# A transformer trunk on one core: context's w2 sums kept in PSUM, the mixing norm of token group 1 taken step by step, raw weights in nineteen tiles

## The chip, the core and the metric

The kernel runs on one core of a Trainium2 chip. The metric is the device time of one execution in microseconds (us), lower is better. The core has TensorE (PE, matrix products; its weight loads are listed as PEld), VectorE (DVE), ScalarE (ACT), GpSimd (POOL), and SyncE (SP), whose queue issues nearly all DMAs. Matrix products add up in PSUM: eight banks of 128 partitions x 512 floats, in two rings of four tiles, psa and psb.

## The reference

One layer of a diffusion backbone on 1024 latent tokens and 256 context tokens, model width 1024, hidden width 2816. Cut to what matters:

```python
x   = x   + 0.5 * m_l[2] * swiglu(modulate(rms_norm(x,   norm1_w), m_l[0], m_l[1]), w1, w3, w2)
ctx = ctx + 0.5 * m_c[2] * swiglu(modulate(rms_norm(ctx, norm1_w), m_c[0], m_c[1]), w1, w3, w2)
y_l, _ = token_mixing(modulate(rms_norm(x, norm2_w), m_l[3], m_l[4]),
                      modulate(rms_norm(ctx, norm2_w), m_c[3], m_c[4]), ...)
x = x + m_l[5] * y_l
x = x + 0.5 * m_l[8] * swiglu(modulate(rms_norm(x, norm3_w), m_l[6], m_l[7]), v1, v3, v2)
return rms_norm(x, final_norm_w)

def swiglu(h, w1, w3, w2):
    return (silu(h @ w1) * (h @ w3)) @ w2
```

Token mixing has retention heads and gated linear attention heads. The retention decay uses `log_sigmoid` of eight numbers per layer.

## The kernel before, in words

Activations lie transposed: x[tg][k] is 128 features x the tokens of group tg. Groups 0 and 1 are 512 latent tokens each, group 2 is the 256 context tokens. Every product is made of three matmuls in a reduced float format: each operand is split into a high part (hi, made by ACT, line 60) and a low part (lo, the rest, by DVE or POOL, line 61), and `mm3` (lines 63 to 67) adds hi x hi, hi x lo and lo x hi.

The first FFN of the latent tokens uses a seven-product scheme: products of hidden blocks are stored to memory (gd), and `back6` and `prod` (lines 466, 493) make the w2 products from them. The last of these, prod(4), is left for later.

Between back6 and prod(4) lies the **context's hidden stage**, the loop at line 1575: eleven passes, each on a pair of hidden blocks f and f + 1, through `classic` (line 621). For each block it loads w1 and w3 in halves of 128 x 512 (`load_halves`, `load_half`, `raw_half`), splits them, makes `H` (line 616: 24 matmuls of 256 columns into one psa bank), then silu (`s1`, ACT), the product (`s3`, DVE), and its split into g. Two pairs of hi and lo tiles of a half are taken from the slots h00 to h07 (`halves_slots`, line 274), in turn. In the middle of each pass `mid2` makes the w2 sums of the pass before: `Y` (line 591) takes four half-weights of w2, split by DVE, and for each of the eight feature blocks six matmuls into a psb bank, after which DVE multiplies by the gate and adds to x[2] (line 600). The w1 and w3 halves' low parts are made by POOL here (CENG). The last sums, Y(20), are put into prod(4) by a plan of steps (`plan`, lines 1505 to 1548), and the context's second norm after them.

All raw weight halves land in a ring of NR = 6 tiles ("raw", line 258). The pool of f1 has another ring, "s", of 19 tiles of the same size (`stile`, line 575), which holds silu's results and the kept products.

In the same passes the norm of token group 1 for the mixing stage is made: `norm2(1, i)` (lines 1516 to 1535). Step 0 sums squares, step 1 sums over features with small matmuls (line 187) and takes the power on POOL, step 2 spreads the result over the partitions with small matmuls (line 203) and copies it, and the steps 3 to 10 write h[1][k]: DVE at line 217, ACT at 218, DVE at 223. One step is handed over after each pass (`pend`), but h[1] is allocated whole ahead of them (line 1572), and its small sums use psb (psN).

After prod(4) come the norm of group 0, the context's keys and values (`ctx_k`, `ctx_v`), and `mix_setup` (line 873), which calls `lg_setup` (line 840): it loads the eight decays, makes log_sigmoid with a power on POOL and a series of some 25 tiny DVE instructions, and from it the tables kd and cdec (ACT). Then the mixing stage, the output projection and the second FFN.

Within each engine the order of the instructions is made by a scheduler that goes by priorities in program order (`high_priority`, `low`) and by its own estimate of when things are ready; at some places an order is fixed by hand. It also assigns the tiles of a ring and adds the waits. Each engine runs its queue in order.

Of the kernel before, what the change touches and what calls it, by code (L numbers as in the profile page):

```python
# [11 lines left out]
F32 = mybir.dt.float32  # L12
F32R = mybir.dt.float32r
AF = mybir.ActivationFunctionType
ALU = mybir.AluOpType
PSUM = bass.MemoryType.PSUM

P = 128
D = 1024
KD = D // P  # L20
DFF = 2816
NF = DFF // P
NP = NF // 2
LAT = 1024
CTX = 256
# [6 lines left out]
class Trunk:  # L32
# [222 lines left out]
                          for k in range(KD)]  # L255

    def raw_half(self, src=None):
        t = self.tile(self.wp, [P, 512], F32, "raw", NR)
        if src is not None:
            t = t[:, :src.shape[1]]  # L260
            self.nc.sync.dma_start(t, src)
        return t
# [11 lines left out]
    def halves_slots(self, i):  # L274
        if i < 2:
            return None, None
        return tuple(self.hslot(f"0{2 * (i % 4) + j}") for j in range(2))

    def load_halves(self, src, dst=(None, None), eng=None):
        return [self.load_half(src[:, 512 * i:512 * i + 512], dst[i], eng) for i in range(2)]  # L280
# [212 lines left out]
    def back6(self, keep=True):  # L493
        A = self.bank4(self.psA)
        self.prod(1, A, True)
        c1 = self.keep4(A)
        B = self.bank4(self.psB)
        self.prod(2, B, True)
        self.add4(0, 0, self.plus4(c1, B))
        self.prod(6, A, False)  # L500
        u2 = self.keep4(A)
        B = self.bank4(self.psB)
        self.prod(5, B, True)
        c5 = self.keep4(B)
        self.prod(7, A, False)
        if keep:
            u3 = self.keep4(A)
            self.add4(1, 1, self.plus4(c5, u3))
        else:
            self.add4(1, 1, self.plus4(c5, A))  # L510
            self.add4(0, 1, A)
        self.prod(3, B, False)
        self.add4(1, 0, self.plus4(u2, B))
        return A
# [54 lines left out]
    def ffn_open(self, i, gates, pool):  # L569
        self.w1, self.w3, self.w2 = (self.I[f"w{i}{j}"] for j in (1, 3, 2))  # L570
        self.gates_m, self.fp, self.s, self.g = gates, pool, {}, {}
        self.gd, self.sd = self.gds[i - 1], self.sds[i - 1]
        self.nraw, self.nslot, self.feed, self.steps, self.held = -1, 0, iter(()), None, None

    def stile(self):
        return self.tile(self.fp, [P, 512], F32, "s", self.ns)
# [14 lines left out]
    def Y(self, f, order, after=None, qs=(0, 1)):  # L591
        nc, g = self.nc, self.g

        def unit(w, tg, o, n, m):
            ps = self.psB()
            for i in range(2):
                self.mm3(ps[:, :n], [t[:, m % 4 * P:(m % 4 + 1) * P] for t in w[i]], [t[:, o:o + n] for t in g[f + i, tg]],
                         i == 0, i == 1)
            x = self.x[tg][m][:, o:o + n]
            nc.vector.scalar_tensor_tensor(out=x, in0=ps[:, :n], scalar=self.gates_m[int(tg == 2)][:, m:m + 1], in1=x,  # L600
                                           op0=ALU.mult, op1=ALU.add)

        ws = {}
        for q in qs:
            ws[q] = [self.load_half(self.w2[f + i][:, 512 * q:512 * q + 512]) for i in range(2)]
            if not after:
                for tg, o, n in order:
                    for m in range(4):
                        unit(ws[q], tg, o, n, 4 * q + m)
        if after:  # L610
            for tg, o, n in order:
                for m in range(KD):
                    unit(ws[m // 4], tg, o, n, m)
                after(tg, o, n)

    def H(self, w, tg):
        ps = self.psA()
        self.proj(w, tg, ps)
        return ps
# [217 lines left out]
            act(a, a, AF.Exp, scale=-1.0)  # L837
            act(a, a, AF.Ln, bias=1.0)

    def lg_setup(self):  # L840
        nc, I, cp = self.nc, self.I, self.cp2
        x = self.tile(cp, [P, 8], F32, "lgx")
        nc.sync.dma_start(x, I["decay"].broadcast_to([P, 8]))
        e = self.tile(cp, [P, 8], F32, "lge")
        nc.vector.memset(e, float(np.e))
        u = self.tile(cp, [P, 8], F32, "lgu")
        nc.vector.tensor_scalar(out=u, in0=x, scalar1=-1.0, scalar2=None, op0=ALU.mult)
        nc.vector.tensor_tensor(out=u, in0=u, in1=x, op=ALU.min)
        nc.gpsimd.tensor_tensor(out=u, in0=e, in1=u, op=ALU.pow)
        t = self.tile(cp, [P, 8], F32, "lgt")  # L850
        nc.vector.tensor_scalar(out=t, in0=u, scalar1=2.0, scalar2=None, op0=ALU.add)
        nc.vector.reciprocal(t, t)
        nc.vector.tensor_tensor(out=u, in0=u, in1=t, op=ALU.mult)
        nc.vector.tensor_tensor(out=t, in0=u, in1=u, op=ALU.mult)
        nc.vector.tensor_scalar(out=e, in0=t, scalar1=1.0 / 19, scalar2=1.0 / 17, op0=ALU.mult, op1=ALU.add)
        for m in (15, 13, 11, 9, 7, 5, 3, 1):
            nc.vector.tensor_tensor(out=e, in0=e, in1=t, op=ALU.mult)
            nc.vector.tensor_scalar(out=e, in0=e, scalar1=1.0 / m, scalar2=None, op0=ALU.add)
        nc.vector.tensor_tensor(out=e, in0=e, in1=u, op=ALU.mult)
        nc.vector.tensor_scalar(out=x, in0=x, scalar1=0.0, scalar2=None, op0=ALU.min)  # L860
        nc.vector.scalar_tensor_tensor(out=x, in0=e, scalar=-2.0, in1=x, op0=ALU.mult, op1=ALU.add)
        self.lg = x
        self.kd = {}
        for i, (nm, s, pos) in enumerate((("f", 0, 2), ("f0", 0, 3), ("b", 4, 0), ("b1", 4, 1))):
            t = self.tile(cp, [P, 4], F32, "kd" + nm)
            nc.vector.tensor_scalar(out=t, in0=x[:, s:s + 4], scalar1=self.tab[:, POSC + pos:POSC + pos + 1],
                                    scalar2=None, op0=ALU.mult)
            nc.scalar.activation(t, t, AF.Exp)
            self.kd[nm] = t
        self.cdec = self.tile(cp, [P, 8], F32, "cdec")  # L870
        nc.scalar.activation(self.cdec, x, AF.Exp, scale=float(P))
# [572 lines left out]
    def run(self):  # L1444
        nc, tc, I = self.nc, self.tc, self.I
        S = {}

        def opn(name, side="left"):
            S[name] = tc.tile_pool(name=name, bufs=1, reuse_waits="tile", side=side)
            return S[name].__enter__()  # L1450
# [9 lines left out]
        xp = opn("xp", "right")  # L1460
        self.x, self.h, self.tr = {}, {}, None
        self.consts()
        warm = self.tile(self.dp, [P, 8], F32, "warm")
        nc.scalar.activation(warm, self.mhalf, AF.Silu)
        self.load_x((xp, xp, None), (0,))
        nc.scalar.activation(self.ccol, self.ccol, AF.Silu)
# [6 lines left out]
        with tc.manual_schedule(engines={mybir.EngineType.PE, mybir.EngineType.DVE, mybir.EngineType.Activation}):  # L1473
            ws = self.first1((xp, xp, None), n1)
# [24 lines left out]
        hc = opn("hc", "right")  # L1499
        self.gp = hc  # L1500
        n2 = opn("n2", "right")
# [3 lines left out]
        plan = defaultdict(list)  # L1505
# [10 lines left out]
        def norm_step(tg, i, a, b):  # L1516
            with self.low(NLOW if tg == 1 and i in (1, 2) else None):
                norm_part(tg, i, a, b)
# [16 lines left out]
        norm2 = lambda tg, i: norm_step(tg, i, self.mcol(4, int(tg == 2)), self.mcol(3, int(tg == 2)))  # L1535
        for i, at in enumerate((24, 27, 30, *range(33, 33 + KD))):
            plan[at].append(lambda i=i: ctx1(i))

        CT = [(2, 0, 256)]
        p4 = 6 * NP  # L1540
        plan[p4 + 1] += [lambda: self.Y(NF - 2, CT), lambda: self.alloc_h((2,), hc), lambda: norm2(2, 0)]
        plan[p4 + 4].append(lambda: norm2(2, 1))
        plan[p4 + 6].append(lambda: norm2(2, 2))
        for k in range(KD):
# [22 lines left out]
        def spill(tg):  # L1567
            o = TGS[tg][0]
            for k in range(KD):
                nc.sync.dma_start(self.xd[k * P:(k + 1) * P, o:o + 512], self.x[tg][k])  # L1570

        self.alloc_h((1,), self.hp)
        norm2(1, 0)
        pend = [lambda i=i: norm2(1, i) for i in range(1, 3 + KD)] + [lambda: spill(1)]
        for f in range(0, NF, 2):
            self.classic(f, (2,), mid2=(lambda: self.Y(f - 2, CT)) if f else None, eng=[nc.gpsimd if e else None for e in CENG])
            pend.pop(0)()
        A = self.bank4(self.psA)
        self.prod(4, A, True)
        self.add4(0, 1, A)  # L1580
# [48 lines left out]
        raw = [self.t34_raw(k) for k in range(4)]  # L1629
# [18 lines left out]
NR = 6  # L1648
# [17 lines left out]
CENG = (1, 1, 1, 1)  # L1666
# [98 lines left out]
```

## Time and profile before

| | us |
|---|---|
| median of 3 runs | 2178.55 |
| lowest and highest run | 2176.82, 2179.85 |
| profiled execution | 2180.54 |
| its span in the profile | 2178.8 |
| PE busy | 2121.3 (97% of the span) |
| DVE busy | 1525.0 (70%) |
| ACT busy | 980.7 (45%) |
| POOL busy | 280.4 (13%) |

The profile is of one execution. A row of a timeline has the start, the length, the engine and line, the operation, the tile written and the tiles read, and in brackets the idle time of the engine ahead of it and what ended that. A row of waits has who waited, for whom, the sum, the count and the longest. A group has its count, the busy time, the mean length of one in ns, and the idle time ahead of it. A table of stages has the busy time of each engine in a stretch, and PEclk, the clock that was granted to TensorE as a share of full speed. Lengths of matmuls are modelled; the pace of PE is read from the distance of their starts.

### The profile page before, as it was taken

Reading aid. Unit: us, or ns where it says so; the run is one execution under the profiler, and the core shown is the slowest. Engines: PE = TensorE matmul, PEld = TensorE weight load, DVE = VectorE, ACT = ScalarE, POOL = GpSimd, SP = SyncE. Lnnn points to the kernel's source line nnn. Section 1 sums busy time; section 2 is a strip of 40 time slices with the busy share of each in tenths; the row PEclk is TensorE's granted clock in tenths of the full one; section 3 lists DMA queues with packets and bytes.
Section 4 is the critical chain, followed back from the end, with each engine's and each line's share of the span. In section 5 each row is a group of like instructions: output and inputs, shape, how many; then the busy total and the mean of one; then the engine's idle time right before and its main releaser. Section 6 shows DMA issues by size and latency. Waiting matters only on the chain. (4 is left out here: it accounts for less than half of the span.)

```text
span 2178.8 us, 32819 instructions
## 1 busy us (share of the span) xinstructions
PE 2121.3 (97%) x11558; PEld 1811.5 (83%) x11558; DVE 1525.0 (70%) x2735; ACT 980.7 (45%) x1811; POOL 280.4 (13%) x285
## 2 busy tenths in 40 slices
PE   8999999999999999999989999999999999999998
PEld 7888888888889999987778988788878888888888
DVE  7889999756766756834665546758777666675676
ACT  4433334345545444546454335425343433444553
POOL 0000000000026562611132113200000000010000
PEclk8999999999999999999999999999999999999999
DMA  9267768469966565553322312324134444467674
GB/s 331 83 231 239 267 221 268 167 221 325 306 210 193 156 183 171 180 152 100 92 65 63 98 57 88 122 83 162 63 120 161 146 160 159 150 217 251 207 241 147
DMA packets 202933, 373.39 MB, mean 171 GB/s; under 512 B 24016, under 2 KB 37264, under 8 KB 202768
## 3 DMA queue, kind: packets, MB, share of 16 engines
q1 hardware_dynamic: 202336, 371.16, 52.7%
q8 instruction: 90, 1.47, 0.3%
q14 instruction: 75, 0.61, 0.1%
q10 hardware_dynamic: 432, 0.13, 0.0%
HBM read 296.72 MB, written 66.09 MB: 167 GB/s over the span
## 5 line engine op out<-in xcount | busy, mean ns | idle before, releaser
L60 ACT ACTIVATE whi<-raw 128x512 fp32r<-128x512 f32 (+1 forms) x563 | 347.1, 622 | 621.1 <-PE psa L66 169.1
L61 DVE TENSOR_TENSOR wlo<-raw,whi 128x512 fp32r<-128x512 f32 (+1 forms) x533 | 368.1, 694 | 314.3 <-ACT whi L60 310.9
L65 PE MATMUL psa<-hh,whi 128*128 128x512 f32 (+1 forms) x1108 | 435.2, 393 | 0.1
L66 PE MATMUL psa<-hl,whi 128*128 128x512 f32 (+1 forms) x1108 | 434.6, 392 | 0.0
L67 PE MATMUL psa<-hh,wlo 128*128 128x512 f32 (+1 forms) x1108 | 434.3, 392 | 0.0
L65 PE MATMUL psb<-hh,whi 128*128 128x512 f32 (+1 forms) x680 | 260.0, 382 | 0.5 <-ACT whi L60 0.5
L67 PE MATMUL psb<-hh,wlo 128*128 128x512 f32 (+1 forms) x680 | 259.7, 382 | 0.6 <-DVE wlo L61 0.6
L66 PE MATMUL psb<-hl,whi 128*128 128x512 f32 (+1 forms) x680 | 259.7, 382 | 0.0
L65 PEld LDWEIGHTS psa<-hh,whi 128*128 128x128 f32 x1108 | 209.1, 189 | 42.1 <-ACT s L341 0.6
L67 PEld LDWEIGHTS psa<-hh,wlo 128*128 128x128 f32 x1108 | 209.0, 189 | 41.7
L66 PEld LDWEIGHTS psa<-hl,whi 128*128 128x128 f32 x1108 | 209.1, 189 | 41.3
L65 PEld LDWEIGHTS psb<-hh,whi 128*128 128x128 f32 x680 | 127.9, 188 | 25.9 <-ACT whi L60 1.0
L67 PEld LDWEIGHTS psb<-hh,wlo 128*128 128x128 f32 x680 | 127.8, 188 | 25.7 <-DVE wlo L61 1.0
L66 PEld LDWEIGHTS psb<-hl,whi 128*128 128x128 f32 x680 | 127.9, 188 | 24.8
L60 ACT ACTIVATE hh<-raw 128x512 fp32r<-128x512 f32 x180 | 110.4, 623 | 72.7 <-PE psa L66 44.3
L61 POOL TENSOR_TENSOR hl<-raw,hh 128x512 fp32r<-128x512 f32 x84 | 116.2, 1393 | 70.5 <-ACT hh L60 64.4
L1095 POOL TENSOR_TENSOR nr<-nr,mhalf 128x4 f32<-128x4 f32 (+1 forms) x11 | 10.6, 964 | 869.3 <-DVE nr L1094 869.3
L65 PE MATMUL psa<-hh,hh 128*128 128x256 f32 x376 | 107.8, 287 | 0.0
L67 PE MATMUL psa<-hh,hl 128*128 128x256 f32 x376 | 107.8, 287 | 0.0
L66 PE MATMUL psa<-hl,hh 128*128 128x256 f32 x376 | 107.8, 287 | 0.0
L66 PE MATMUL psa<-wlo,hh 128*128 128x256 f32 (+1 forms) x320 | 93.8, 293 | 1.6 <-DVE wlo L61 1.5
L65 PE MATMUL psa<-whi,hh 128*128 128x256 f32 (+1 forms) x320 | 93.5, 292 | 1.2 <-ACT s L1049 1.2
(402 smaller groups left out, 4251.7 us busy)
## 6 DMA issues: line engine op xcount, KB each, us to landing
raw<-in_w SPq DMA_DIRECT2D x374, 256.0 KB, 3.2
gd<-s SPq DMA_DIRECT2D x154, 256.0 KB, 2.8
ada<-in_adaT SPq DMA_DIRECT2D x76, 512.0 KB, 4.8
raw<-gd SPq DMA_DIRECT2D x91, 256.0 KB, 3.0
s<-in_w SPq DMA_DIRECT2D x66, 256.0 KB, 5.0
sd<-s SPq DMA_DIRECT2D x44, 256.0 KB, 2.9
raw<-sd SPq DMA_DIRECT2D x44, 256.0 KB, 3.1
hh<-in_w SPq DMA_DIRECT2D x44, 256.0 KB, 3.9
```

Of the source, the lines that this page charges most:

```text
L60: nc.scalar.activation(hi, src, AF.Copy)
L61: (eng or nc.vector).tensor_tensor(out=lo, in0=src, in1=hi.bitcast(F32), op=ALU.subtract)
L65: mm(ps, wa[0], xa[0], start=start, stop=False, skip_group_check=more)
L66: mm(ps, wa[0], xa[1], start=False, stop=False, skip_group_check=more)
L67: mm(ps, wa[1], xa[0], start=False, stop=stop, skip_group_check=more)
L1095: nc.gpsimd.tensor_tensor(out=r, in0=r, in1=self.mhalf[:, :n], op=ALU.pow)
```

## The change

Four things are changed.

- `Yc` takes the place of `Y` for the context. It holds all four psb banks from the first pass to the last, two sums of 256 columns in each, and adds the matmuls of all passes there. Only the last call (f = 20) multiplies by the gate and adds to x[2].
- The norm of group 1: its small sums use psa in this stage, and h[1][k] is allocated in its own step, in the slot h1k. In the passes 2 to 9 the last half-weight of w3 uses the slot of the step that follows, in place of h07.
- While `deep` is set (the eleven passes), raw halves land in the ring "s" of 19 tiles in place of the ring "raw" of 6.
- The first part of `lg_setup`, up to the logarithm, is now `lg_start`: it is called after the fifth pass (f = 8), with tiles in the norm's pool, and its result is kept in eight columns of mod that are no longer used by then.

The tile "warm" at the start is 64 columns wide in place of 8, which puts the tiles of x in the first stage 224 bytes lower.

```diff
     def raw_half(self, src=None):
-        t = self.tile(self.wp, [P, 512], F32, "raw", NR)
+        t = self.stile() if self.deep else self.tile(self.wp, [P, 512], F32, "raw", NR)
...
     def halves_slots(self, i):
         if i < 2:
             return None, None
-        return tuple(self.hslot(f"0{2 * (i % 4) + j}") for j in range(2))
+        p, last = i // 4, i % 4 == 3
+        return tuple(self.hslot(f"1{p - 2}" if last and j and 2 <= p < 10 else f"0{2 * (i % 4) + j}") for j in range(2))
...
+    def Yc(self, f):
+        if not f:
+            self.yb = self.bank4(self.psB)
+        ws = {q: [self.load_half(self.w2[f + i][:, 512 * q:512 * q + 512]) for i in range(2)] for q in range(2)}
+        for m in range(KD):
+            ps = self.yb[m // 2][:, m % 2 * CTX:(m % 2 + 1) * CTX]
+            for i in range(2):
+                self.mm3(ps, [t[:, m % 4 * P:(m % 4 + 1) * P] for t in ws[m // 4][i]], self.g[f + i, 2],
+                         not (f or i or m % 2), f == NF - 2 and i == 1, True)
+            if f == NF - 2:
+                x = self.x[2][m]
+                self.nc.vector.scalar_tensor_tensor(out=x, in0=ps, scalar=self.gates_m[1][:, m:m + 1], in1=x,
+                                                    op0=ALU.mult, op1=ALU.add)
...
-    def lg_setup(self):
-        nc, I, cp = self.nc, self.I, self.cp2
+    def lg_start(self, cp):
+        nc, I = self.nc, self.I
...
-        nc.vector.scalar_tensor_tensor(out=x, in0=e, scalar=-2.0, in1=x, op0=ALU.mult, op1=ALU.add)
-        self.lg = x
+        self.lg = self.mcol(0, 1)
+        nc.vector.scalar_tensor_tensor(out=self.lg, in0=e, scalar=-2.0, in1=x, op0=ALU.mult, op1=ALU.add)
+
+    def lg_setup(self):
+        nc, cp, x = self.nc, self.cp2, self.lg
...
-        warm = self.tile(self.dp, [P, 8], F32, "warm")
+        warm = self.tile(self.dp, [P, 64], F32, "warm")[:, :8]
...
-        CT = [(2, 0, 256)]
         p4 = 6 * NP
-        plan[p4 + 1] += [lambda: self.Y(NF - 2, CT), lambda: self.alloc_h((2,), hc), lambda: norm2(2, 0)]
+        plan[p4 + 1] += [lambda: self.Yc(NF - 2), lambda: self.alloc_h((2,), hc), lambda: norm2(2, 0)]
...
-        self.alloc_h((1,), self.hp)
+        self.h[1] = []
         norm2(1, 0)
-        pend = [lambda i=i: norm2(1, i) for i in range(1, 3 + KD)] + [lambda: spill(1)]
+
+        def norm1(k):
+            self.h[1].append(self.hslot(f"1{k}"))
+            norm2(1, 3 + k)
+
+        self.psN, self.deep = self.psA, True
+        pend = [lambda i=i: norm2(1, i) for i in (1, 2)] + [lambda k=k: norm1(k) for k in range(KD)] + [lambda: spill(1)]
         for f in range(0, NF, 2):
-            self.classic(f, (2,), mid2=(lambda: self.Y(f - 2, CT)) if f else None, eng=[nc.gpsimd if e else None for e in CENG])
+            self.classic(f, (2,), mid2=(lambda: self.Yc(f - 2)) if f else None, eng=[nc.gpsimd if e else None for e in CENG])
             pend.pop(0)()
+            if f == 8:
+                self.lg_start(n2)
+        self.psN, self.deep = self.psB, False
```

More of the change, by code (lines that the diff above doesn't have):

```diff
@@ L572, in ffn_open @@
         self.gd, self.sd = self.gds[i - 1], self.sds[i - 1]
-        self.nraw, self.nslot, self.feed, self.steps, self.held = -1, 0, iter(()), None, None
+        self.nraw, self.nslot, self.feed, self.steps, self.held, self.deep = -1, 0, iter(()), None, None, False
     def stile(self):
```

## The prediction

> **What bounds the kernel now.** I read the page first, then the table of stages, then the list of what TensorE (PE) waited for, then PE's own rows at each hole.
>
> ```profile
> span 2178.8 us, 32819 instructions
> PE 2121.3 (97%) x11558; PEld 1811.5 (83%) x11558; DVE 1525.0 (70%) x2735; ACT 980.7 (45%) x1811; POOL 280.4 (13%) x285
> ...
> 660.00:680.00 20.00, 17.40 (x143) 16.99 (x142) 11.01 (x19) 10.62 (x22) 16.06 (x11) 1.00 0.65 199
> 680.00:700.00 20.00, 20.00 (x145) 20.00 (x144) 10.71 (x20) 8.62 (x16) 11.25 (x9) 0.83 0.57 177
> 700.00:720.00 20.00, 16.32 (x119) 16.12 (x118) 18.11 (x28) 9.17 (x17) 7.55 (x5) 0.85 0.41 119
> 720.00:740.00 20.00, 18.90 (x152) 18.49 (x152) 18.91 (x26) 10.62 (x20) 12.28 (x8) 0.98 0.51 154
> 740.00:760.00 20.00, 20.00 (x170) 20.00 (x168) 9.63 (x18) 9.24 (x18) 11.89 (x9) 1.00 0.61 189
> ```
>
> PE is the bound, and only its holes and its slow stretches can be won back. Each row of the table gives the stretch, its length, the busy time (and count) of PE, PEld, DVE, ACT and POOL, PE's granted clock, and the DMA share. The context's hidden stage lies here. In 740:760 PE does 170 matmuls in 20 us; in the four rows before it does 143, 145, 119 and 152. Two things are seen: idle time (660:680, 700:720, 720:740), and a granted clock of 0.83 and 0.85 where PE counts as busy and yet does fewer matmuls. DVE is at 18 and 19 of 20 in the last two of the four.
>
> ```profile
> PE psb L65 <- DVE x L600: 7.3, 4, 3.7
> PE psa L66 <- DVE wlo L61: 1.5, 2, 1.2
> ```
>
> All waits of PE for the additions of line 600 (each empties one w2 bank into x) come to 7.3 us in four holes. PE's rows show them, and the ends of the stage:
>
> ```profile
> 648.70 0.28 PE L65 MATMUL psa<-hh,whi 128*128 128x256 f32 x1
> ...
> 673.15 0.28 PE L67 MATMUL psb<-ghi,wlo 128*128 128x256 f32 x1
> 674.15 0.39 PE L65 MATMUL psb<-ghi,whi 128*128 128x256 f32 x1 [0.72 <-DVE x L600]
> ...
> 677.01 0.28 PE L67 MATMUL psb<-ghi,wlo 128*128 128x256 f32 x1
> 679.17 0.39 PE L65 MATMUL psb<-ghi,whi 128*128 128x256 f32 x1 [1.88 <-DVE x L600]
> ...
> 711.20 0.28 PE L67 MATMUL psb<-ghi,wlo 128*128 128x256 f32 x1
> 715.15 0.58 PE L65 MATMUL psb<-ghi,whi 128*128 128x256 f32 x1 [3.67 <-DVE x L600]
> ...
> 734.88 0.28 PE L67 MATMUL psb<-ghi,wlo 128*128 128x256 f32 x1
> 736.15 0.39 PE L65 MATMUL psb<-ghi,whi 128*128 128x256 f32 x1 [0.99 <-DVE x L600]
> ...
> 848.80 0.28 PE L67 MATMUL psa<-hh,hl 128*128 128x256 f32 x1
> 848.92 0.40 PE L65 MATMUL psa<-hh,whi 128*128 128x512 f32 x1
> ```
>
> The first 256-wide matmul starts at 648.70, and the first 512-wide one of prod(4) at 848.92: 200.2 us. Matmuls that wait for nothing start 0.12 us apart (848.80, 848.92). The code has 24 matmuls for each H, four H a pair, eleven pairs: 1056; and 48 for the w2 sums of each of the ten pairs that end before prod(4): 480. That is 1536 x 0.12 = 184.3 us, so 15.9 us are lost. Starts lie 1.00, 2.16, 3.95 and 1.27 apart at the holes, less 0.12 each: **7.9 us of waits**.
>
> ```profile
> 685.40 0.41 PE L65 MATMUL psa<-hh,hh 128*128 128x256 f32 x1
> 685.62 0.41 PE L66 MATMUL psa<-hl,hh 128*128 128x256 f32 x1
> ...
> 707.71 1.78 DVE L223 SCALAR_TENSOR_TENSOR hl<-nt,modl,hh 128x512 fp32r<-128x512 f32 x1
> 709.53 1.67 DVE L217 SCALAR_TENSOR_TENSOR nt<-x,modl,nrb 128x512 f32<-128x512 f32 x1
> 711.12 0.68 DVE L61 TENSOR_TENSOR wlo<-raw,whi 128x512 fp32r<-128x512 f32 x1
> 712.72 1.64 DVE L223 SCALAR_TENSOR_TENSOR hl<-nt,modl,hh 128x512 fp32r<-128x512 f32 x1
> 714.62 1.26 DVE L600 SCALAR_TENSOR_TENSOR x<-psb,modc,x 128x256 f32<-128x256 f32 x3
> ```
>
> The slow stretches follow the holes. 0.83 over 20 us is 0.17 x 20 / 0.5 = 6.8 us at half clock; 0.85 is 6.0, and 0.98 the last 0.8 of the same spell, which so ran from 714.0 to 720.8 and had work from 715.15: 5.65 us. There matmuls start 0.22 apart (685.40, 685.62) against 0.12, so 0.10/0.22 of the time is lost: 3.1 + 2.6 = **5.7 us of slow clock**. The DVE rows show whom the longest wait was for: three additions at 714.62, queued behind the norm of token group 1. From 740 on the additions still run, the norm doesn't, and PE holds its pace: it is the two together that stop it.
>
> **The change part by part.** *Sums kept in PSUM.* The matmuls are as many as before. Of the additions eight are left, behind pair 10:
>
> ```profile
> L600 DVE SCALAR_TENSOR_TENSOR x<-psb,modc,x 128x256 f32<-128x256 f32 x88 | 38.7, 474 | 2.8 <-PE psb L67 2.7
> L61 POOL TENSOR_TENSOR hl<-raw,hh 128x512 fp32r<-128x512 f32 x80 | 110.7, 1393 | 70.5 <-ACT hh L60 64.4 <-PE psa L66 2.8
> ```
>
> 80 x 0.474 = 37.9 us leave DVE, and no sum waits for a bank before the last. So the 7.9 us go, and the 5.7 us of slow clock that follow them. What is late next? By the list, nothing: PE's only waits in this stage are these.
>
> *The norm spread.* Its eight steps must now each wait for the pair whose last half-weight uses the same slot: one step a pair, two DVE instructions of up to 1.78 us (707.71) in a pair's 17.3 (144 x 0.12). A step's ACT part can wait for PE's last reads of that slot; the next weight splits queue behind it on ACT, and behind the step's second half on DVE. ACT is busy 9.2 of 20 us at 740:760, which hides a wait of some microseconds; uncovered, it is rival 2. Its sums move from psb to psa, where H has four banks of 24 x 0.12 = 2.9 us each; three are left for a moment, which I cost at nothing. They still take PE's time:
>
> ```profile
> 670.77 0.28 PE L66 MATMUL psa<-hl,hh 128*128 128x256 f32 x1
> 670.89 0.28 PE L187 MATMUL psb<-ones,nacc 128*128 128x1 f32 x2
> 671.03 0.36 PE L65 MATMUL psb<-ghi,whi 128*128 128x256 f32 x1
> 671.24 0.28 PE L66 MATMUL psb<-glo,whi 128*128 128x256 f32 x1
> ```
>
> 671.24 would be 671.01 without that pair of small matmuls: 0.23 us; four such, and four of line 203 taken alike, are 1.8 us, which stay. 7.9 + 5.7 + 1.8 = 15.4 of the 15.9 lost; of the 0.5 left, slow restarts after the holes, I take 0.4 as gained too. **Context: -14.0 us.**
>
> *Raw weights in nineteen tiles.* No load is added; each is issued earlier. No wait of PE here names a load or a split, so I take nothing: below, nothing to gain; above, the slower rival.
>
> *The decay logarithm (lg_start) in pair 4.*
>
> ```profile
> 932.87 1.78 POOL L849 TENSOR_TENSOR lgu<-lge,lgu 128x8 f32<-128x8 f32 x1 [5.42 <-DMA crv<-s]
> 934.69 0.93 DVE L851 TENSOR_SCALAR lgt<-lgu 128x8 f32<-128x8 f32 x1 [1.53 <-POOL lgu L849]
> 937.41 0.40 PE L66 MATMUL psa<-wlo,hh 128*128 128x288 f32 x1 [1.18 <-DVE wlo L61]
> 941.03 0.21 ACT L871 ACTIVATE cdec<-lgx 128x8 f32<-128x8 f32 x1 [7.63 <-DVE lgx L861]
> ```
>
> The weight split that PE awaits at 937.41 stood in DVE's queue behind this chain, which itself awaited POOL's power. Both are done some 200 us earlier then (pair 4 ends near 648.7 + 5 x 17.3 = 735): **-1.2 us**. ACT's wait of 7.63 goes too; if splits behind it are late as well the part gives 2.4, and if PE finds the next wait at once, 0. In its new place it queues some 25 short DVE instructions, a small load on SP, and 1.78 us on POOL, whose 80 low parts fill 111 of 200 us: hidden; at worst one low part (1.39) comes 1.8 late.
>
> *x's tiles 224 bytes lower, the log's place in mod's columns:* no instruction more; nothing.
>
> *What is planned anew.* The order behind this stage is made by a scheduler and can fall otherwise. The mixing stage shows what that is worth:
>
> ```profile
> 980.00:1000.00 20.00, 17.41 (x111) 15.13 (x110) 9.73 (x21) 13.71 (x24) 8.60 (x17) 0.91 0.31 89
> ```
>
> 2.6 us idle and 3.6 us at half clock (1.6 lost): one such stretch more or less is 4.2 us either way. I take 0, and keep the ends.
>
> **Sum.** The profiled execution took 2180.54 us (span and 1.74 around it), 0.09% above the median of 2178.55. 14.0 + 1.2 = 15.2; the last eight additions and the log's new place may cost some tenths, say 0.6: 14.6. From the median, **2164 us**.
>
> **Rivals.** *1. The banks' halves take turns.* Each bank now holds two sums. In the last pass DVE empties the one half while PE would write the other. If they may not overlap, PE waits four times: its last matmul drains (0.28 - 0.12), DVE adds (0.474), two hand-overs at some 0.06: 0.75 each, 3.0 in all, and by the first spell a slow stretch of 2.6: 2169.6. For: nothing splits the halves. Against: prod(4) and the other three banks offer PE other work. [...]
>
> *2. The wait passes on.* DVE's low parts of the w2 weights (711.12) stand behind the same norm steps. If the sums now wait for these, once: 3.8 + 2.6 back, 2170.4 (chance 0.13); at both spells 2176 (0.05). For: norm steps of 1.7 us stay. Against: one step a pair, and those weights are split well before their use.
>
> *3. A spell of its own.* If the first slow stretch is not the holes' doing, it stays: 2167. For: the holes before it are only 1.0 and 2.2 long. Against: at 740:760, with as many matmuls and no hole, the clock is 1.00. [...]
>
> *4. Slower: the loads shut out their own stage.* Silu's results and the raw weights now share nineteen tiles, and SP's queue is in order. If early raw tiles hold all, a result or a w2 load that is needed now waits, PE with it. Priced by the worst hole, 3.8 + 2.6 = 6.4 us each; the gain is gone at the third, and with four it is 2164 + 25.6 = 2189.6. Against: twelve loads and two live results a pair are fewer than nineteen.
>
> *5. It doesn't do what it says:* the norm is not spread. Then DVE jams as at 707 to 714 now, but no sum waits for DVE: 2164 too; folded into the forecast.
>
> **How the numbers follow.** Forecast 0.56 (its own range 2159 to 2169), rival 1 0.13, rival 2 0.13 and 0.05, rival 3 0.08, rival 4 0.05. The low end is 2164 less the 4.2 and some of the 1.2 that the log may give; the high end takes in rivals 1 to 3 at one spell: 2159 to 2172. 0.2% is 4.4 us, about what a measurement of this kernel can tell. Faster: 0.56 + 0.13 + 0.13 + 0.08 = 0.90; same 0.05 (2176); slower 0.05.
>
> **What would show it.** Right: no wait for line 600 but in the last pass; from the first 256-wide matmul to prod(4) 186 to 187 us; a clock of 1.00 throughout it; no wait at the first weights of the mixing stage for the log. Wrong: a hole in that stage that names a low part (2), a load or a silu tile (4), a slow stretch without holes (3), or four holes at the last sums (1).

## The result, and the profile after

The changed kernel takes **2239.59 us** (median of 4 runs, 2238.63 to 2240.97) against 2178.29 before (4 runs): a ratio of 1.0277, 95% interval 1.0264 to 1.029. It is 61 us slower; the forecast was 14.6 us faster. The profiled execution has a span of 2239.2 us against 2178.8.

All of it lies in context's hidden stage. First the stages of the changed kernel that stand for the five shown of before (columns as there: busy time and count of PE, PEld, DVE, ACT, POOL; PE's granted clock; DMA share; GB/s):

```profile
660.00:680.00 20.00, 16.48 (x98) 15.49 (x97) 7.29 (x10) 7.31 (x15) 9.74 (x8) 0.76 0.51 175
680.00:700.00 20.00, 17.58 (x140) 16.99 (x139) 5.76 (x9) 5.18 (x11) 7.10 (x6) 0.98 0.46 145
700.00:720.00 20.00, 17.09 (x124) 16.48 (x125) 7.52 (x9) 6.98 (x15) 10.40 (x8) 0.91 0.38 116
720.00:740.00 20.00, 16.59 (x120) 15.78 (x118) 7.59 (x10) 7.64 (x17) 7.25 (x6) 0.91 0.47 149
740.00:760.00 20.00, 17.73 (x131) 17.33 (x132) 7.80 (x10) 6.47 (x13) 9.86 (x8) 0.91 0.52 158
```

Before, PE did 170 matmuls in 740:760 and kept that pace to the end. Now no stretch reaches it, while DVE and ACT are busy for less of the time than before in each of the five, and the DMA share is lower: the engines wait for each other. Whom PE waits for, in the whole run:

```profile
PE psa L65 <- ACT hh L60: 24.2, 21, 4.2
PE psa L67 <- POOL hl L61: 17.1, 20, 0.9
PE psa L65 <- ACT whi L60: 6.0, 1, 6.0
```

The waits for the additions are gone, as forecast. In their place stand two waits a block for the high and the low part of its own weights, one of 6 us at the stage's start and one of 4.17 us at its end. PE's rows show the ends of the stage, and one of its pairs:

```profile
645.24 0.28 PE L65 MATMUL psa<-hh,whi 128*128 128x256 f32 x1
...
654.28 0.58 PE L65 MATMUL psa<-hh,whi 128*128 128x256 f32 x1 [6.01 <-ACT whi L60]
...
761.29 0.28 PE L67 MATMUL psa<-hh,hl 128*128 128x256 f32 x1
762.56 0.39 PE L65 MATMUL psa<-hh,hh 128*128 128x256 f32 x1 [0.99 <-ACT hh L60]
762.78 0.28 PE L66 MATMUL psa<-hl,hh 128*128 128x256 f32 x1
763.96 0.39 PE L67 MATMUL psa<-hh,hl 128*128 128x256 f32 x1 [0.90 <-POOL hl L61]
764.18 0.28 PE L65 MATMUL psa<-hh,hh 128*128 128x256 f32 x1
...
770.72 0.39 PE L65 MATMUL psa<-hh,hh 128*128 128x256 f32 x1 [0.99 <-ACT hh L60]
...
772.12 0.39 PE L67 MATMUL psa<-hh,hl 128*128 128x256 f32 x1 [0.90 <-POOL hl L61]
...
908.18 0.58 PE L65 MATMUL psa<-hh,hh 128*128 128x256 f32 x1 [4.17 <-ACT hh L60]
...
908.77 0.63 PE L65 MATMUL psa<-hh,whi 128*128 128x512 f32 x1
```

From the first 256-wide matmul to prod(4) it is now 263.5 us (645.24 to 908.77), before 200.2: 63.3 more. The stage starts 3.5 us earlier, and from prod(4) to the end there is 0.5 us more (1330.4 against 1329.9): 63.3 - 3.5 + 0.5 = 60.3, the difference of the spans but for rounding. One pair, from an instruction of ACT to the same one of the next pair, after and before:

```profile
761.61:785.17 23.56, 19.78 (x144) 18.97 (x144) 7.80 (x10) 8.45 (x18) 10.83 (x8) 0.93 0.44 135
```

```profile
759.77:777.05 17.28, 17.28 (x147) 17.28 (x146) 8.71 (x16) 8.42 (x17) 10.89 (x9) 1.00 0.62 183
```

The loss of 6.28 us a pair can be added up from the rows: starts 1.27, 0.22, 1.18 and 0.22 apart at each of two places (761.29 to 764.18, and alike to 772.35), less 0.12 each, are 2 x 2.41 = 4.8; a clock of 0.93 over 23.56 us is 3.3 us at half clock, 1.5 of it lost. Not every pair is alike (one of the later ones has no slow clock), but eleven at this rate would be 69 us; with the 6.0 us at the start and the 4.2 at the end that is about the 79.2 that are lost in 263.5.

**The row that explains it** is not PE's but ACT's. Its waits in 700 to 900, after (all but one of 0.8 us) and then before (three of its rows; the stage ends at 848.92 there):

```profile
ACT s L582 <- PE psa L67: 71.6, 16, 7.4
ACT hh L218 <- PE psa L66: 26.1, 8, 4.1
ACT ghi L60 <- DVE s L588: 23.7, 8, 3.2
ACT hh L60 <- PE psa L66: 1.8, 1, 1.8
```

```profile
ACT hh L60 <- PE psa L66: 38.3, 24, 4.9
ACT whi L60 <- DMA raw<-in_w: 10.5, 8, 1.6
ACT s L581 <- PE psa L67: 1.3, 2, 1.0
```

Before, ACT waited in front of a *split* (hh, line 60), for PE to be done with the old weights in that slot: it split as early as a slot allowed. Now it waits in front of a *silu*, up to 7.4 us, for PE to finish the block; and no wait of ACT names a DMA, so the raw weights behind that silu are there. ACT and POOL around one silu:

```profile
761.61 0.38 ACT L582 ACTIVATE s<-psa 128x256 f32<-128x256 f32 x1 [7.23 <-PE psa L67]
761.89 2.18 ACT L60 ACTIVATE hh<-s 128x512 fp32r<-128x512 f32 x4
```

```profile
762.64 5.03 POOL L61 TENSOR_TENSOR hl<-s,hh 128x512 fp32r<-128x512 f32 x4 [6.84 <-ACT hh L60]
```

ACT stands idle for 7.23 us with four splits behind the silu. PE ends the block at 761.29 and has nothing until the first of these four is made (762.56), then until POOL has the low part (763.96). The three engines work in turn. The rows show ACT's queue in order: 7.23 us idle ahead of a silu, with four splits behind it that wait for no load.

The weight splits of ACT in the order of its queue as the program was built, around a silu of the second block of a pair (a split of a product is left out, and the slot's number of each hh; the number that is left counts up in the order of the program):

```
changed kernel                          kernel before
hh_1496 <- s_6806    w1 of this block   hh_1640 <- raw_7372  w1, one pair later
hh_1498 <- s_6810    w1 of this block   hh_1642 <- raw_7376  w1, one pair later
silu s_6839 <- psa_6814                 silu s_7151 <- psa_7126
hh_1504 <- s_6845    w3 of this block   hh_1648 <- raw_7411  w3, one pair later
hh_1506 <- s_6849    w3 of this block   hh_1650 <- raw_7415  w3, one pair later
```

Before, the weights split next to a silu are those of a whole pair later; now they are the block's own. What has to be shown is why the order changed.

### The profile page after: what moved, and what is told of

Its sections match the earlier page's. It is cut to its first block, busy times and chain, and to the rows that moved or that the text cites. A ratio compares the mean times of both kernels' runs of the same rounds, so it can differ in the third digit from the quotient of the medians.

```text
span 2239.2 us, 32700 instructions
## 1 busy us (share of the span) xinstructions
PE 2143.0 (96%) x11558; PEld 1826.0 (82%) x11558; DVE 1496.7 (67%) x2655; ACT 975.7 (44%) x1811; POOL 275.2 (12%) x285
## 5 line engine op out<-in xcount | busy, mean ns | idle before, releaser
L60 ACT ACTIVATE whi<-raw 128x512 fp32r<-128x512 f32 (+1 forms) x519 | 320.4, 622 | 606.5 <-PE psa L66 169.0
L61 DVE TENSOR_TENSOR wlo<-raw,whi 128x512 fp32r<-128x512 f32 (+1 forms) x493 | 337.4, 688 | 280.1 <-ACT whi L60 275.8
L67 PEld LDWEIGHTS psb<-hh,wlo 128*128 128x128 f32 x680 | 127.8, 188 | 26.1 <-DVE wlo L61 1.4
L65 PE MATMUL psa<-hh,hh 128*128 128x256 f32 x376 | 116.6, 310 | 24.2 <-ACT hh L60 24.2
L67 PE MATMUL psa<-hh,hl 128*128 128x256 f32 x376 | 117.3, 312 | 17.2 <-POOL hl L61 17.1
L61 POOL TENSOR_TENSOR hl<-s,hh 128x512 fp32r<-128x512 f32 x84 | 113.7, 1375 | 139.0 <-ACT hh L60 103.9
L66 PE MATMUL psa<-hl,hh 128*128 128x256 f32 x376 | 113.9, 303 | 0.0
L65 PEld LDWEIGHTS psa<-hh,hh 128*128 128x128 f32 x376 | 80.2, 213 | 28.4 <-ACT hh L60 28.4
L67 PEld LDWEIGHTS psa<-hh,hl 128*128 128x128 f32 x376 | 80.0, 213 | 22.8 <-POOL hl L61 22.6
L588 DVE TENSOR_TENSOR s<-psa,s 128x256 f32<-128x256 f32 x22 | 9.3, 422 | 128.4 <-PE psa L67 126.7
```

Of the source, the lines that this page charges most:

```text
L60: nc.scalar.activation(hi, src, AF.Copy)
L61: (eng or nc.vector).tensor_tensor(out=lo, in0=src, in1=hi.bitcast(F32), op=ALU.subtract)
L65: mm(ps, wa[0], xa[0], start=start, stop=False, skip_group_check=more)
L66: mm(ps, wa[0], xa[1], start=False, stop=False, skip_group_check=more)
L67: mm(ps, wa[1], xa[0], start=False, stop=stop, skip_group_check=more)
L588: self.nc.vector.tensor_tensor(out=u, in0=src[:, :n], in1=u, op=ALU.mult)
```

## The experiments

**Theory A.** Silu's results and the raw halves now take tiles of *one* ring, and a ring gives its tiles out in the order of the program. The load of a block's w3 stands in the program behind the block's silu, so the scheduler can't place it, nor its split, ahead of that silu, however many tiles are free. (This is the order of the plan. On the chip the load has landed by then, as the rows above show; but its split stands in ACT's queue where the plan put it.) **Rival B:** the norm steps of group 1 hold ACT up (its 26.1 us of waits in line 218). **Rival C:** nineteen tiles let the loads run too far ahead. Twelve runs, in two groups; "stage" is from the first 256-wide matmul to prod(4) of the profiled execution (200.2 before, 263.5 after), and the ratio is against the kernel before on the same chip.

| run | median us | ratio, 95% interval | stage us |
|---|---|---|---|
| e1_short_ring | 2187.18 | 1.0043, 1.0028 to 1.0058 | 207.7 |
| e2_silu_apart | 2181.66 | 1.0014, 1.0005 to 1.0024 | 199.4 |
| e3_before_ring | 2250.42 | 1.0337, 1.0321 to 1.0353 | 267.1 |
| e4_norm_whole | 2243.47 | 1.0305, 1.0286 to 1.0323 | 262.2 |
| e5_sums_only | 2173.36 | 0.9984, 0.9973 to 0.9996 | 193.7 |
| e6_norm_only | 2182.62 | 1.0025, 1.0012 to 1.0038 | 202.9 |
| e7_loads_ahead | 2175.48 | 0.9989, 0.9976 to 1.0002 | 194.5 |
| e8_shared_six | 2243.70 | 1.0299, 1.0273 to 1.0324 | 263.7 |
| e9_norm_later | 2174.18 | 0.9973, 0.9964 to 0.9983 | 194.6 |
| e10_sums_log | 2172.07 | 0.9963, 0.9950 to 0.9977 | 194.1 |
| e11_ahead_whole | 2173.66 | 0.9975, 0.9965 to 0.9986 | 196.1 |
| e12_ahead_later | 2169.74 | 0.9957, 0.9942 to 0.9973 | 191.4 |

### What made it slow: e1 to e4, e7, e8

**e1: the changed kernel with the raw ring of 6.**

```diff
-        self.psN, self.deep = self.psA, True
+        self.psN, self.deep = self.psA, False
```

> The changed kernel with one thing undone: in context's hidden stage the raw halves land in the ring raw of 6 tiles again, not in silu's ring of 19. Theory A (sharing one ring with silu's results is the loss: a weight split now stands behind the silu ahead of it on ACT): all of the 61 us and the forecast gain come back, 2160 to 2170 us, 17.3 us a pair, and PE waits for no high part of line 60 but at the stage's start. Rival B (the norm steps of group 1, which now wait on ACT for PE's last reads of their slot, 26.1 us in eight waits, hold the splits up): still 2225 to 2240. Rival C (19 tiles let loads run so far ahead that they crowd the DMA queues): as A here.

Measured: ratio 1.0043. 52 of the 61 us are back (2239.6 - 2187.2), the stage from 263.5 to 207.7, and no wait for hh of line 60 is left. Rival B falls as the main cause. But the forecast gain did not come with it: that is the second question below.

**e2: nineteen tiles for the raw halves, silu's results in the idle ring of 6.**

```diff
-        t = self.stile()[:, :n]
+        t = (self.tile(self.wp, [P, 512], F32, "raw", NR) if self.deep else self.stile())[:, :n]
         self.nc.scalar.activation(t, ps[:, :n], AF.Silu)
```

> The changed kernel, raw halves still in the ring of 19, but silu's results of this stage in the ring raw of 6, which is idle there: the same 19 tiles for the loads, and nothing shared. Theory A (sharing): 2160 to 2170 us, as with the short ring. Rival B (norm steps in slots): 2225 to 2240. Rival C (loads run too far ahead): 2225 to 2240, as nothing holds them back.

Measured: 1.0014, with all the nineteen tiles for loads. Rival C falls: depth does no harm. What did it is that the two share, in this order of the program. The size was missed by 12 us, and one place holds most of it, at the stage's start (PE's row; the clock is 0.74 at 660:680):

```profile
666.75 0.58 PE L65 MATMUL psb<-ghi,whi 128*128 128x256 f32 x1 [6.74 <-ACT ghi L60]
```

**e3: the kernel before with the shared ring alone.**

```diff
     def raw_half(self, src=None):
-        t = self.tile(self.wp, [P, 512], F32, "raw", NR)
+        t = self.stile() if self.deep else self.tile(self.wp, [P, 512], F32, "raw", NR)
...
+        self.deep = True
         for f in range(0, NF, 2):
...
+        self.deep = False
         A = self.bank4(self.psA)
```

> The kernel before with one thing added: raw halves in silu's ring of 19 in context's hidden stage; sums in x, the norm in a lump, the logarithm late, all as before. Theory A (sharing): some 24 us a pair in place of 17.3, so 2235 to 2255 us. Rival B (norm steps in slots, of which there are none here): 2175 to 2182. Rival C: slow too.

Measured: 1.0337, 72 us slower than before, in the range of theory A. ACT shows the same sign, with neither the sums nor the norm changed (700 to 900):

```profile
ACT s L581 <- PE psa L67: 70.9, 16, 7.3
```

**e4: the changed kernel with the norm in a lump, no slot of its own for a step.**

```diff
-        p, last = i // 4, i % 4 == 3
-        return tuple(self.hslot(f"1{p - 2}" if last and j and 2 <= p < 10 else f"0{2 * (i % 4) + j}") for j in range(2))
+        return tuple(self.hslot(f"0{2 * (i % 4) + j}") for j in range(2))
...
-        self.h[1] = []
+        self.alloc_h((1,), self.hp)
         norm2(1, 0)
...
-        pend = [lambda i=i: norm2(1, i) for i in (1, 2)] + [lambda k=k: norm1(k) for k in range(KD)] + [lambda: spill(1)]
+        pend = [lambda i=i: norm2(1, i) for i in range(1, 3 + KD)] + [lambda: spill(1)]
```

> The changed kernel with the norm of group 1 as before: h allocated whole, every last half-weight of w3 in slot h07 again, no norm step in a slot of its own; the shared ring of 19 stays. Theory A (sharing): 2228 to 2240 us, the norm's part no more than 10 us of the loss. Rival B (norm steps in slots): 2160 to 2180, PE's waits for line 60 gone. Rival C: as A.

Measured: 1.0305, as slow as the changed kernel. So the 26.1 us in which ACT waited at norm steps cost nothing that shows: rival B falls here too.

**e7: the shared ring, but each half asked for ten halves earlier in the program.**

```diff
     def raw_half(self, src=None):
-        t = self.stile() if self.deep else self.tile(self.wp, [P, 512], F32, "raw", NR)
+        if self.deep:
+            while self.seq and len(self.got) < 10:
+                t = self.stile()
+                self.nc.sync.dma_start(t, self.seq.popleft())
+                self.got.append(t)
+            return self.got.popleft()
+        t = self.tile(self.wp, [P, 512], F32, "raw", NR)
...
+        self.got, self.seq = deque(), deque()
```

(`seq` is then filled with the halves of the eleven passes in the order of their use.)

> The changed kernel, the shared ring of 19 kept for raw halves and silu's results, but each raw half is asked for ten halves earlier in the program, so that it takes its tile ahead of the silu results of its own and the blocks before. Theory A (a ring gives out its tiles in program order, so a load and its split are ordered behind the silu that stands ahead of them in the program): 2172 to 2192 us, near the kernels with rings apart (2181.7 and 2187.2). If it is the number of tiles, or two users in one ring as such: 2225 to 2245.

**e8: silu's results and the raw halves share the ring of 6.**

```diff
-        t = self.stile()[:, :n]
+        t = (self.tile(self.wp, [P, 512], F32, "raw", NR) if tg == 2 else self.stile())[:, :n]
         self.nc.scalar.activation(t, ps[:, :n], AF.Silu)
...
-        self.psN, self.deep = self.psA, True
+        self.psN, self.deep = self.psA, False
```

> The changed kernel with raw halves in the ring raw of 6 as before, and silu's results of context in that same ring: shared again, with 6 tiles in place of 19. Theory A (program order of a shared ring): 2230 to 2270 us, a pair 23 us or more. If the 19 tiles were what made it slow: 2180 to 2192, as with the short ring alone (2187.2).

Measured: e7 0.9989, e8 1.0299. The two are a cross: nineteen shared tiles with the loads ahead in the program are as fast as before; six shared tiles in the changed kernel's order are as slow as nineteen (stage 263.7 against 263.5). ACT's wait at the silu in 700 to 840, e7 and then e8:

```profile
ACT s L588 <- PE psa L67: 32.2, 14, 4.6
```

```profile
ACT raw L582 <- PE psa L67: 52.0, 12, 7.5
```

(e8's silu results have the name raw.) ACT's idle time at a silu is thus not the loss by itself: e7 still has 32.2 us of it, but the splits behind those silus are again of later blocks, and PE has no wait for hh in e7's stage. What counts is whose weights stand behind the silu. So it is the place of the requests in the program, in a ring that both share, and neither the count of tiles nor the sharing as such. That the scheduler gives tiles out in program order is inferred from these runs; its own records were not seen.

### Where the forecast gain is: e5, e6, e9 to e12

**e5: the kernel before with the sums in PSUM alone** (`Yc` as in the change, in the passes and for the last sums).

```diff
+        self.psN = self.psA
         pend = [lambda i=i: norm2(1, i) for i in range(1, 3 + KD)] + [lambda: spill(1)]
         for f in range(0, NF, 2):
-            self.classic(f, (2,), mid2=(lambda: self.Y(f - 2, CT)) if f else None, eng=[nc.gpsimd if e else None for e in CENG])
+            self.classic(f, (2,), mid2=(lambda: self.Yc(f - 2)) if f else None, eng=[nc.gpsimd if e else None for e in CENG])
             pend.pop(0)()
+        self.psN = self.psB
```

> The kernel before with the first part of the change alone: w2 sums kept in PSUM (and the norm's small sums in psa, since psb is full); norm in a lump, raw ring of 6, logarithm late. The prediction's step (the additions of line 600 hold PE 7.9 us and bring 5.7 us of slow clock): 2164 to 2170 us. Rival D (the stage starts short of split weights, because loads and splits of its first two pairs are late; the additions only stood where PE would have waited anyway): 2176 to 2182, with PE waiting for ghi, glo or whi in the first 40 us in place of x.

Measured: 0.9984, 3.5 us faster (0.9 to 5.9): between the two. The stage is 193.7 against 200.2. The four waits for the additions are gone, the long one at 715 among them, with the norm still in a lump; one wait took the place of the first two. The run gains less than the stage: the profiled execution starts it 0.85 us later, and the part behind it is 2.2 us longer, which was not followed up. PE's only long wait in the stage, and DVE ahead of it:

```profile
665.17 0.58 PE L65 MATMUL psb<-ghi,whi 128*128 128x256 f32 x1 [3.95 <-ACT ghi L60]
```

```profile
655.00 2.48 DVE L481 TENSOR_TENSOR s<-psb,s 128x512 f32<-128x512 f32 x4
657.39 2.73 DVE L487 SCALAR_TENSOR_TENSOR x<-s,modl,x 128x512 f32<-128x512 f32 x4
660.04 0.68 DVE L178 TENSOR_TENSOR nacc<-nacc,nsq 128x512 f32<-128x512 f32 x1
...
664.26 0.41 DVE L587 TENSOR_TENSOR s<-psa,s 128x256 f32<-128x256 f32 x1
```

The product of the first block (664.26) stands in DVE's queue behind the last product before the stage, the additions of x, the squares of the norm and the low parts of w2 between them; the first w2 sums need it. Behind this hole the clock is 0.83 in 660:680; at 700:720, where it was 0.85 before, it is 1.00:

```profile
660.00:680.00 20.00, 15.95 (x111) 15.15 (x110) 9.84 (x16) 9.11 (x19) 9.01 (x7) 0.83 0.62 195
700.00:720.00 20.00, 20.00 (x167) 19.81 (x166) 15.97 (x21) 12.18 (x22) 12.11 (x9) 1.00 0.55 162
```

**e6: the kernel before with the norm spread alone** (e4's diff the other way round, on the kernel before).

> The kernel before with the second part alone: the norm of group 1 spread over the passes, a slot a step; w2 sums added into x as before, raw ring of 6. The prediction's step (the norm's lump on DVE is what the hole of 3.67 us and its 2.6 us of slow clock wait for): 2170 to 2174 us. Rival E (a norm step now waits on ACT for PE's last reads of its slot, and the splits behind it are late): 2182 to 2195.

Measured: 1.0025, 5 us *slower*. PE's waits for the additions are not gone but spread as well, 8.8 us in seven against 7.3 in four (640 to 910):

```profile
PE psb L65 <- DVE x L601: 8.8, 7, 3.5
```

What a spread step does is best seen in e1, where the sums are in PSUM (ACT's rows, DVE's, then PE's, all of one pair):

```profile
798.91 1.67 ACT L60 ACTIVATE hh<-raw 128x512 fp32r<-128x512 f32 x3 [5.65 <-DMA raw<-in_w]
800.49 0.36 ACT L582 ACTIVATE s<-psa 128x256 f32<-128x256 f32 x1
```

```profile
802.09 1.88 DVE L223 SCALAR_TENSOR_TENSOR hl<-nt,modl,hh 128x512 fp32r<-128x512 f32 x1 [0.78 <-ACT hh L218]
803.89 1.48 DVE L61 TENSOR_TENSOR glo<-s,ghi 128x256 fp32r<-128x256 f32 x1
```

```profile
805.42 0.39 PE L66 MATMUL psb<-glo,whi 128*128 128x256 f32 x1 [2.33 <-DVE glo L61]
```

The second half of the step waits for ACT and then takes 1.88 us, and the split of the product (glo), for which PE's next sums wait, stands right behind it. PE has such waits for glo six times in e1's stage, 8.7 us in all. But the step is not alone: the silu that this product needs (800.49) stands behind splits that waited 5.65 us for a load, and in 700 to 840 ACT waits 62.0 us for loads in e1, against 10.5 in the kernel before. How much of the price is the step's and how much the late loads' is not shown here.

**e9: e5 with the last four squares of the norm handed over after the first pass** (each later step of the norm comes one pass later with them).

```diff
-        norm2(1, 0)
-        pend = [lambda i=i: norm2(1, i) for i in range(1, 3 + KD)] + [lambda: spill(1)]
+        pend = [lambda i=i: norm2(1, i) for i in range(2 + KD)] + [lambda: (norm2(1, 2 + KD), spill(1))]
```

> Sums in PSUM alone (as in the run of that part, 2173.4 us), and the last four squares of group 1's norm handed over after the first pass in place of before it. Theory D (the one hole left, 3.95 us for ghi at 665 and the 3.1 us of slow clock behind it, is DVE's crowd at the stage's start: four additions of the product before, four of x, four squares, the low parts of w2, and only then silu's product): some 2 us of squares out of the way, hole 1 to 2.5 us, 2168 to 2172. If the loads alone set that hole: 2172 to 2176.

Measured: 0.9973, not to be told from e5 by the intervals. The hole went from 665 to 683 and was hardly shorter, 3.38 for ghi. There ghi stands on ACT behind a split that waits for its load:

```profile
682.25 0.63 ACT L60 ACTIVATE hh<-raw 128x512 fp32r<-128x512 f32 x1 [1.63 <-DMA raw<-in_w]
682.79 0.40 ACT L60 ACTIVATE ghi<-s 128x256 fp32r<-128x256 f32 x1
```

So the squares were one of two covers: with the ring of 6, the loads are late there too.

**e10: the changed kernel with the ring of 6 and the norm in a lump** (e1 and e4 together: sums in PSUM, the logarithm early, x's tiles lower).

> The changed kernel with the raw ring of 6 and the norm in a lump: left of the change are the sums in PSUM, the logarithm after pass 5 and x's tiles 224 bytes lower. The prediction's step for the logarithm: 1.2 us under the sums alone, 2171 to 2173. Against the kernel with the short ring and the norm spread (2187.2) this run gives the price of spreading the norm where sums are in PSUM: the prediction said a gain, the run of the norm alone says a loss of some 4 us; I expect 10 to 14.

Measured: 0.9963, 8 us faster than before. Against e1 (1.0043) only the norm differs: spreading it costs 0.8%, 17 us, with the ring of 6, more than expected; PE's waits for glo are 0.8 us here, 8.7 there. Against e5 the intervals overlap: the logarithm gives nothing that can be told. PE's row fits that:

```profile
926.37 0.40 PE L65 MATMUL psa<-whi,hh 128*128 128x288 f32 x1 [1.29 <-ACT s L1066]
```

The wait of 1.18 us for the weights' low part behind the logarithm is gone; a wait of 1.29 for a result of ACT (line 1066) stands a little ahead of its place. From 640 to 990, PE's waits for such a result and for such low parts of weights come to 2.8 us here and to 2.7 in the kernel before (2.0 in e5).

**e11 and e12: loads ten halves ahead and the norm in a lump (the edits of e7 and e4); e12 with the squares later too (that of e9).**

> The kernel with loads asked for ten halves ahead in the shared ring (2175.5 us), and the norm in a lump again. If spreading the norm costs where splits run ahead too: 2165 to 2172. If it costs only with the ring of 6: 2173 to 2178.

> As the run before it in this list (loads ten halves ahead, norm in a lump), with the last four squares of group 1's norm after the first pass. Theory D: a further 1 to 3 us, 2163 to 2171, the best of all; if the squares are not what the start waits for: no change.

Measured: e11 0.9975, no better than e10; e12 **0.9957** (0.9942 to 0.9973), some 9 us faster than before and 70 than the changed kernel, the fastest of all by its median, though the intervals of e9 to e11 overlap with its own. e11's interval also overlaps with e7's, from which only the norm parts it: with the loads ahead, spreading the norm costs nothing that can be told. Three stretches of e12:

```profile
660.00:680.00 20.00, 19.99 (x167) 19.79 (x166) 9.57 (x11) 11.14 (x23) 15.81 (x11) 1.00 0.98 332
680.00:700.00 20.00, 20.00 (x169) 20.00 (x169) 9.11 (x12) 7.39 (x15) 11.72 (x9) 1.00 0.68 219
700.00:720.00 20.00, 17.52 (x135) 17.32 (x134) 10.64 (x12) 10.06 (x20) 10.80 (x8) 0.91 0.48 148
```

With both covers off, late loads and squares, the hole of the stage's start and its slow clock are gone. The loads were the larger cover: with these ahead and the squares in their old place, PE's longest wait in the first 40 us of the stage is 1.33 us in e7 and 1.05 in e11. The longest wait that is left in e12 is at 700:720, a wait for the diagonal that the norm's small matmuls of line 203 use, with its own slow clock:

```profile
PE psa L203 <- DVE ndiag L194: 2.5, 1, 2.5
```

Of the 15.9 us that the stage lost before, 7.1 are lost still (191.4 - 184.3).

## Why the prediction was wrong

**The step that failed is "Raw weights in nineteen tiles": "No wait of PE here names a load or a split, so I take nothing."** It is true that none did; but that was so because the splits ran a pair ahead, and the change took just that away. I asked whether loads would come late and counted tiles. I did not ask what else takes tiles from that ring, in which order, and so behind which instruction a split would stand on ACT. What the runs showed in place of the nothing: 52 us in the changed kernel (to e1) and 72 in the kernel before (e3).

**Rival 4 had the place but not the mechanism.** It said that the shared ring could make the stage shut its loads out, at 6.4 us each, and set against it that "twelve loads and two live results a pair are fewer than nineteen". That count does not bear on it: with six tiles it is as slow (e8), with nineteen and the loads asked for earlier it is not (e7). The price was not one long hole now and then but four short ones in every pair, 6.28 us with the slow clock. The prediction's signs would have misled, too: no hole names a load or a silu tile, its sign of rival 4, and every second one names a low part, its sign of rival 2.

**Context, -14.0 us, was mis-sized.** The sums in PSUM alone took 6.5 us out of the stage, 3.5 out of the run (e5). The waits for line 600 did go (7.9), and the second slow spell with them. But at the stage's start PE needs the first products as much as the free banks, and these are late for another reason: DVE's crowd, and behind it the loads (e9, e7, e11). That is rival 2's pattern, a wait passed on; it passed to the split of the product and not, as I wrote, to the low parts of w2. "By the list, nothing" was the error: a list of waits names who came last, and not who would have come next.

**The spread norm, costed at nothing, costs with six tiles.** 0.25% alone (e6), 0.8% with the sums in PSUM (e10 to e1); with the loads ahead nothing that can be told (e11 to e7). I looked at ACT's wait for the slot, which the 9.2 of 20 us on ACT were to hide, and wrote in passing that splits queue "on DVE behind the step's second half". That half sentence is a part of the price, as e1's rows show; late loads stand beside it, and how the two share it stays open. The small sums in psa, also put at nothing, are where e7, e11 and e12 have their wait of 2.5 us at line 203; the list names the diagonal from DVE there and not a bank. The lump did no harm once no sum waits for DVE, as rival 5 said: e5 keeps a clock of 1.00 at 700:720 with the norm in it.

**The logarithm, -1.2:** by PE's rows its lower bound, "if PE finds the next wait at once, 0", is what happened. By the times of e10 and e5, 1.2 us can't be told from 0.

**Rivals 1 and 3.** In the changed kernel PE has no wait for an addition in the last pass, so the banks' halves cost nothing there; e2 shows one such wait, of 0.90 us, and e8 one of 0.50, where rival 1 had four of 0.75. The slow spells went where the holes went (e12 has none up to 700), so no spell was seen without holes; but the tie is loose, as the last section shows.

**x's tiles 224 bytes lower** was not tried by itself; e10, which has it, is not slower than e5, which has not.

## What to carry to other kernels

When a buffer is moved into a ring that something else uses, look not at the number of tiles but at who asks for tiles between two of its requests in program order: whatever waits in that place now stands ahead of the load and, in an engine's queue, of all that follows from it (here a silu ahead of which ACT stood idle for 7.23 us, with four splits behind it). Ask for the loads earlier in the program, or give each user its own ring. And a wait that is missing from a list because work runs ahead is the first thing that a change of buffers can bring back: check for each engine in front of which instruction it idles, and whether that changes.

## What the runs showed of the hardware

From 660 to 903 of the changed kernel PE was never idle for more than 1.20 us at a time, and yet its clock halved in nearly every pair. Around 772 (columns as in the tables of stages), and a pair in which it didn't:

```profile
769.00:771.00 2.00, 1.01 (x9) 0.81 (x7) 0.34 (x1) 1.23 (x3) 0.20 (x1) 1.00 0.72 204
771.00:773.00 2.00, 1.10 (x9) 0.90 (x9) 1.26 (x2) 2.00 (x5) 2.00 (x2) 0.98 0.19 72
773.00:775.00 2.00, 2.00 (x11) 2.00 (x11) 2.00 (x2) 0.78 (x2) 1.85 (x2) 0.50 0.57 150
775.00:777.00 2.00, 2.00 (x14) 2.00 (x13) 1.46 (x3) 0.00 (x1) 0.46 (x1) 0.67 0.83 284
...
808.74:831.09 22.35, 18.54 (x144) 17.52 (x144) 7.73 (x10) 8.45 (x18) 10.85 (x8) 1.00 0.46 142
```

PE is busy for 2.1 of 4 us, in pieces, and the clock then drops for some 3.3 us. The pair of 808.74 has four holes of the same lengths (1.27 and 1.17, twice), keeps a clock of 1.00 and takes 22.35 us in place of 23.56. The start of the stage shows the same: e11 has holes of 0.63, 0.52, 1.02 and 0.50 us within 4 us and then a clock of 0.50 at 660:662, while e7, with 0.70, 0.50, 0.50 and 1.61 us within 5 us, keeps 1.00. So behind short holes close together the clock halved in some places and not in others; what decides between the two is not shown. In the kernel before, the slow spells came with holes of 1.88 (679.17) and 3.67 us (715.15); from 660 to 903 of the changed kernel the clock halved with none over 1.20.
